# Another PSUM bank for the head outputs, a written TensorE order for the early projections, and fewer weight rests on GpSimd in a two-layer decoder trunk

## The chip, the cores and the metric

The kernel runs on one core of one Trainium2 chip. The metric is the device time of one execution in microseconds (us), less is better. Three executions of the kernel before took 598.71, 599.31 and 599.65 us; their median is 599.31 us.

## The reference

A pre-norm decoder trunk of two layers, batch 1, 256 positions, width 1024, all float32. The even layer projects the normed input once and feeds two groups of heads: A, latent attention (eight heads; a compressed query of 256 and a compressed key/value of 128 columns are normed and projected up, with a rotary part of 32 columns), and B, dilated attention (eight heads of 64). Their outputs go through one output projection. The odd layer is grouped-query attention with a window of 128 and learned sinks (16 query heads, 2 key/value heads). A SwiGLU feed-forward layer of 2816 follows each; a norm ends the trunk.

```python
for layer in range(DEPTH):
    hn = _rmsnorm(h, attn_norm[layer])
    if layer % 2 == 0:
        mix = _even_mixer(hn, ...)   # oA: latent, oB: dilated; concatenate @ w_out
    else:
        mix = _odd_mixer(hn, ...)    # grouped query heads with sinks
    h = h + mix
    h = h + _swiglu(_rmsnorm(h, ffn_norm[layer]), f_w_gate_up[layer], f_w_down[layer])
return _rmsnorm(h, final_norm)
```

In `_even_mixer`, `c_q` and `c_kv` are the first 384 columns of the input projection; `_rmsnorm(c_q) @ w_uq` gives the queries (`pq` in the kernel), `_rmsnorm(c_kv) @ w_ukv` the keys and values (`pk`, `pv`).

## The kernel before, in words

Positions stand on the 128 partitions, in two row blocks `b`. To keep float32 precision, each factor of a product is split in a rounded part `hi` and a **rest** `lo`, and one product is three matmuls (`mm3`, L116): hi·hi (L124), hi·lo (L125), lo·hi (L126), each 128x512 for most weights. A product of this kind is a *job* below.

**Weights** are loaded in units of up to 1 MB into `raw`, three buffers in turn (`load`, L55, on SyncE's queue). `part_weight` (L80) then cuts each unit into parts of up to 512 columns: ScalarE casts `hi` (L93), and `rest` (L73) picks VectorE or GpSimd for the subtraction that makes `lo` (L94). For the seven weights named in `POOLED` (L70) every third rest goes to VectorE and the others to GpSimd; all other rests are VectorE's. `hi` and `lo` lie in seven pairs of buffers.

**Even layer, early part.** `pc` is the product for the latent columns. For each `b` (L231 on): a mean square of the row of `h` gives `rstd_n`, two more of `pc` give `rstd_c` (ScalarE, VectorE, GpSimd in turn), VectorE forms the normed `cg` (L244), TensorE transposes it (`cT`, L252), and a split follows. The dilated projection is a list `bjobs` of 48 jobs, 16 for each of q, k and v; units 0 and 1 of the weight `b` belong to q, 2 and 3 to k, 4 and 5 to v. The first 24 are traced at L307, then `pq`, `pk` and `pv` for each `b`, with the rotary step on `qA` by VectorE for the first half of the heads and by GpSimd for the second (L326 to L331).

**Attention** (`attention`, L452) goes over pairs of heads: four latent (two sets of turns each), four dilated, and eight grouped in the odd layer. Turn `i` of the loop holds: the scores of pair i; the transposes of q and k of pair i+1 (`T`, L433); the transposes of the probabilities of pair i−1 (`pT`, L405), one head after the other; and the head output of pair i−1 (`o`, L416), which is split into `oT`. The remaining jobs fill the places between (`other`, L457): of each share 20, 40 and 60% have been done at the three first places, and the rest at the fourth.

**PSUM** has eight banks. Four (`acc`) rotate for projections; four have names and are used by attention, one buffer each: `s0` and `s1` hold scores (`s0` also the second `pT`), `p` the first `pT`, and `t` both `T` and `o`:

```python
pp = att(("p", "s0")[i], f"pT_{self.name}{i}")   # L403, turn_p
po = att("t", f"o_{self.name}")                  # L410, values
pt = att("t", f"T_{name}")                       # L431, transposes
```

**Order.** A planner orders each engine's instructions by readiness in its own model and by program order. Inside `tc.manual_schedule(engines={PE})` TensorE's order is the one written; before, that held for the two attention loops and the ends of the output projections, not for the early part.

Of the kernel before, what the change touches and what calls it, by code (L numbers as in the profile page):

```python
# [11 lines left out]
F32 = mybir.dt.float32  # L12
F32R = mybir.dt.float32r
# [3 lines left out]
P = 128  # L17
# [23 lines left out]
def trunk(ctx: ExitStack, tc: tile.TileContext, dr):  # L41
    nc = tc.nc
# [24 lines left out]
                between()  # L67
        st["raw"].append((raw, width, cut, u))

    POOLED = {"b", "ukv", "uq", "wo0", "kv", "qc", "wo1"}  # L70
    pooled = [0]

    def rest(name):  # L73

        if name not in POOLED:
            return nc.vector
        pooled[0] += 1
        return nc.vector if pooled[0] % 3 == 0 else nc.gpsimd

    def part_weight(name, between=None):  # L80

        _, n, kts = dr[name]
        st = streams[name]
        raw, width, cut, u = st["raw"].pop(0)
        per = n * kts
        for i in range(width // per):
            hi = wpool.tile([P, 1024], F32R, tag="wh", name=f"wh_{name}_{u}_{i}")
            lo = wpool.tile([P, 1024], F32R, tag="wl", name=f"wl_{name}_{u}_{i}")
            step = min(per, cut, 512 if per == 1024 else 416)
            for a in range(0, per, step):  # L90
                e = min(per, a + step)
                part = raw[:, i * per + a : i * per + e]
                nc.scalar.copy(hi[:, a:e], part)  # L93
                rest(name).tensor_sub(lo[:, a:e], part, hi[:, a:e].bitcast(F32))  # L94
                if between and a == 0 and i == 0:
                    between()
            st["pieces"].append(Piece(hi, lo, n))
# [129 lines left out]
    load("ukv")  # L227
    nc.sync.dma_start(rope, dr["rope"].rearrange("p (b t f) -> p b t f", b=2, t=3))
    nc.sync.dma_start(mask, dr["mask"])
    cT, kr = [], []  # L230
    for b in range(2):  # L231
        rstd.append(row_rstd(b, "n0"))
        sc = small.tile([P, 2], F32, tag="sc", bufs=2, name=f"sc{b}")
        for j, n in enumerate((256, 128)):
            nc.vector.tensor_scalar_mul(sc[:, j : j + 1], rstd[b], 1.0 / math.sqrt(n))
        ms = small.tile([P, 2], F32, tag="ss2", name=f"ssc{b}")
        mean_squares(pc[b][:, 0:256], sc[:, 0:1], ms[:, 0:1], f"cq{b}")
        mean_squares(pc[b][:, 256:384], sc[:, 1:2], ms[:, 1:2], f"ckv{b}")
        r = rsqrt_eps(ms, f"c{b}")
        r2 = small.tile([P, 2], F32, tag="r2", bufs=2, name=f"r2{b}")  # L240
        nc.vector.tensor_scalar_mul(r2, r, rstd[b])
        cg = big.tile([P, 512], F32, tag="big", name=f"cg{b}")
        for j, (a, e) in enumerate(((0, 256), (256, 384))):
            nc.vector.scalar_tensor_tensor(  # L244
                out=cg[:, a:e], in0=pc[b][:, a:e], scalar=r2[:, j : j + 1], in1=gqkv[:, a:e],
                op0=ALU.mult, op1=ALU.mult,
            )
        c = small.tile([P, 32], F32, tag="krn", bufs=2, name=f"krn{b}")
        nc.scalar.activation(c, pc[b][:, 384:416], AF.Copy, scale=rstd[b])
        pt = any_att(f"cT{b}")  # L250
        for j in range(3):
            nc.tensor.transpose(pt[:, j * P : (j + 1) * P], cg[:, j * P : (j + 1) * P], ident)  # L252
        hi = big.tile([P, 512], F32R, tag="big", name=f"cTh{b}")
        lo = big.tile([P, 512], F32R, tag="big", name=f"cTl{b}")
        split(pt[:, :384], hi[:, :384], lo[:, :384])
        cT.append((hi, lo))
        krb = small.tile([P, 32], F32, tag="kr", bufs=2, name=f"kr{b}")
        t = [small.tile([P, 16], F32, tag="krt", bufs=4, name=f"krt{b}{i}") for i in range(2)]
        cos, nsin, sin = (rope[:, b, i, 0:16] for i in range(3))
        x1, x2 = c[:, 0:16], c[:, 16:32]  # L260
        nc.gpsimd.tensor_mul(krb[:, 0:16], x1, cos)
        nc.gpsimd.tensor_mul(krb[:, 16:32], x2, cos)
        nc.gpsimd.tensor_mul(t[0], x2, nsin)
        nc.gpsimd.tensor_mul(t[1], x1, sin)
        nc.gpsimd.tensor_add(krb[:, 0:16], krb[:, 0:16], t[0])
        nc.gpsimd.tensor_add(krb[:, 16:32], krb[:, 16:32], t[1])
        kr.append(krb)
# [36 lines left out]

    qkvB = [[None, None] for _ in range(3)]
    bjobs = project("b", lambda j: 4 * j, 2, range(3), qkvB, rstd, "b", (2,))
    for f in bjobs[:24]:  # L307
        f()

    qA = [[None, None], [None, None]]  # L310
# [2 lines left out]
    for b in range(2):  # L313
        for half in range(2):
            pq = acc(f"pq{b}{half}")
            for kt in range(2):
                mm3(pq[:, :384], ckt(b, kt), piece("uq", kt).at(0, half * 384, (half + 1) * 384), kt == 0, kt == 1)
            t = big.tile([P, 512], F32, tag="big", name=f"qA{b}{half}")
            qA[b][half] = t[:, :384].rearrange("p (h f) -> p h f", f=96)
            nc.scalar.copy(t[:, :384], pq[:, :384])  # L320
            r = qA[b][half]
            x1, x2 = r[:, :, 64:80], r[:, :, 80:96]
            cos, nsin, sin = (rope[:, b, i, :].rearrange("p (h f) -> p h f", f=16) for i in range(3))
            eng = nc.gpsimd if half else nc.vector
            tt = [work.tile([P, 4, 16], F32, tag="ropet", bufs=4, name=f"ropet{b}{half}{i}") for i in range(2)]
            eng.tensor_mul(tt[0], x2, nsin)  # L326
            eng.tensor_mul(tt[1], x1, sin)
            eng.tensor_mul(x1, x1, cos)
            eng.tensor_mul(x2, x2, cos)
            eng.tensor_add(x1, x1, tt[0])  # L330
            eng.tensor_add(x2, x2, tt[1])  # L331
        pk = acc(f"pk{b}")
        mm3(pk, ckt(b, 2), piece("ukv", 0).at(0, 0, 512), True, True)
        for half in range(2):
            t = big.tile([P, 512], F32, tag="big", name=f"kA{b}{half}")
            kA[b][half] = t[:, :384].rearrange("p (h f) -> p h f", f=96)
            nc.scalar.copy(
                kA[b][half][:, :, 0:64],
                pk[:, half * 256 : (half + 1) * 256].rearrange("p (h f) -> p h f", f=64),
            )  # L340
            nc.vector.tensor_copy(kA[b][half][:, :, 64:96], kr[b].unsqueeze(1).to_broadcast([P, 4, 32]))
        pv = acc(f"pv{b}")
        mm3(pv, ckt(b, 2), piece("ukv", 0).at(0, 512, 1024), True, True)
        vA[b] = [big.tile([P, 512], F32R, tag="big", name=f"vA{p}{b}") for p in "hl"]
        split(pv, *vA[b])

# [12 lines left out]
    class Pair:  # L361
# [45 lines left out]
            split(pp[:, :384], hi, lo)  # L407

        def values(self, kt):
            po = att("t", f"o_{self.name}")  # L410
            out = po.rearrange("p (i q) -> p i q", i=2)
            ph, pl = (t.rearrange("p (i q) -> p i q", i=2) for t in self.p)
            for b, q in ((0, slice(0, 256)), (1, slice(256, 384))):
                vh, vl = self.v(b)
                for j, (x, y) in enumerate(((vh, ph), (vl, ph), (vh, pl))):
                    nc.tensor.matmul(  # L416
                        out[:, :, 128 * b : 256], x, y[:, :, q], start=b == 0 and j == 0, stop=b == 1 and j == 2)
            o = big.tile([P, 512], F32R, tag="big", name=f"oT_{self.name}")
            for i in range(2):
                rows = slice(64 * i, 64 * i + 64)  # L420
                split(po[rows, 256 * i : 256 * i + 256], o[rows, 0:256], o[rows, 256:512])
            oT[kt] = o
# [29 lines left out]
    def attention(pairs, fill):  # L452


        n = len(pairs)

        def other(i, part):  # L457
            share = fill[i]
            cuts = [round(len(share) * x) for x in (0, 0.2, 0.4, 0.6, 1)]
            for f in share[cuts[part] : cuts[part + 1]]:  # L460
                f()

        with tc.manual_schedule(engines={mybir.EngineType.PE}):
            for t in pairs[0].turns():
                t()
            for i in range(n + 1):
                ahead = pairs[i + 1].turns() if i + 1 < n else []
                if i < n:
                    pairs[i].scores()
                other(i, 0)  # L470
                for t in ahead[:1]:
                    t()
                if i > 0:
                    pairs[i - 1].turn_p(0)
                other(i, 1)
                for t in ahead[1:]:
                    t()
                if i > 0:
                    pairs[i - 1].turn_p(1)
                other(i, 2)  # L480
                other(i, 3)
                if i > 0:
                    pairs[i - 1].values(i - 1)

# [352 lines left out]
```

## Time and profile before

| | |
|---|---|
| median of three runs | 599.31 us (598.71 to 599.65) |
| the profiled execution's own time | 599.46 us |
| its span | 597.7 us |
| mean granted TensorE clock | 0.989 of full speed |
| HBM read | 100.02 MB |

The profile names engines PE (TensorE), PEld (its weight loads), DVE (VectorE), ACT (ScalarE), POOL (GpSimd) and SP (SyncE). An idle time in brackets is that of the engine just before the instruction, with what ended it. A row that merges several instructions has the time from the first start to the last end. Ends of matmuls are modelled, so the distance between starts says more than a duration. The stages: early part to about 55 us, even attention to 126, first feed-forward layer to 316, qkv of the odd layer to 340, odd attention to 400, second feed-forward layer to the end.

### The profile page before, as it was taken

The numbers are of one execution on the slowest core, as the hardware profiler recorded it, in microseconds if no ns is written. First come the engines' busy times: TensorE is split into PE (matmuls) and PEld (weight loads), VectorE is DVE, ScalarE is ACT, GpSimd is POOL, SyncE is SP. The second block draws the span as 40 slices with busy tenths as digits, with TensorE's granted clock in tenths as the row PEclk, the third lists the DMA queues.
The fourth block names the chain that finished last, engine by engine and source line by source line (L and its number), as shares of the span: only waits on it lengthen the run. The fifth ranks groups of instructions, "written<-read, shape, count | busy, mean of one in ns | idle before, by whom it ended". The sixth has DMA issues, their size and how long they took to land.

```text
span 597.7 us, 7692 instructions
## 1 busy us (share of the span) xinstructions
PE 567.3 (95%) x2661; PEld 461.5 (77%) x2661; DVE 354.3 (59%) x723; ACT 337.9 (57%) x732; POOL 120.4 (20%) x182
## 2 busy tenths in 40 slices
PE   7877998999999999999999899899999999999995
PEld 5655877778888888888888677778888888888884
DVE  5367467787566556554447566778655655554424
ACT  5666678665554555544338677757555555553412
POOL 1697654200000000000037675211000000000000
PEclk9997999999999999999999999999999999999998
DMA  8846525326645545546544634224654554655401
GB/s 257 333 146 250 187 70 178 106 71 247 210 150 204 200 162 202 183 170 212 192 160 144 241 126 167 81 71 138 250 197 161 205 180 173 211 166 188 140 1 70
DMA packets 18183, 101.57 MB, mean 170 GB/s; under 512 B 2272, under 2 KB 3168, under 8 KB 7520
## 3 DMA queue, kind: packets, MB, share of 16 engines
q1 hardware_dynamic: 17712, 100.55, 49.2%
q10 hardware_dynamic: 432, 0.53, 0.2%
q8 instruction: 21, 0.34, 0.2%
q14 instruction: 18, 0.15, 0.1%
HBM read 100.02 MB, written 1.05 MB: 169 GB/s over the span
## 4 chain that ended last, share of the span: by engine, by line
PE 79%; DVE 7%; ACT 5%; DMA 3%; issue 3%; POOL 1%; SPq 0%; POOLq 0%; DVEq 0%; ACTq 0%
PE f1g L126 7%; PE f0g L126 7%; PE f1g L124 7%; PE f0g L124 7%; PE f0g L125 7%; PE f1g L125 7%; PE f0d L124 3%; PE f0d L126 3%; PE f0d L125 3%; PE f1d L126 3%; PE f1d L124 3%; PE f1d L125 3%; DMA raw_b<-in_w_b_dram 2%; PE p L124 2%; PE p L125 2%
## 5 line engine op out<-in xcount | busy, mean ns | idle before, releaser
L94 DVE TENSOR_TENSOR wl_gu<-raw_gu,wh_gu 128x512 fp32r<-128x512 f32 x176 | 115.4, 688 | 68.3 <-ACT wh_gu L93 66.6
L93 ACT CAST wh_gu<-raw_gu 128x512 fp32r<-128x512 f32 x176 | 102.2, 619 | 77.8 <-PE f1g L126 34.7
L94 DVE TENSOR_TENSOR wl_dn<-raw_dn,wh_dn 128x512 fp32r<-128x512 f32 x88 | 57.5, 689 | 54.8 <-ACT wh_dn L93 54.7
L93 ACT CAST wh_dn<-raw_dn 128x512 fp32r<-128x512 f32 x88 | 50.8, 619 | 61.6 <-PE f1d L126 23.3
L124 PE MATMUL f0g<-wh_gu,hTh_p 128*128 128x512 f32 x176 | 69.8, 396 | 0.0
L124 PE MATMUL f1g<-wh_gu,hTh_p 128*128 128x512 f32 x176 | 69.7, 396 | 0.0
L126 PE MATMUL f1g<-wh_gu,hTl_p 128*128 128x512 f32 x176 | 68.8, 391 | 0.0
L126 PE MATMUL f0g<-wh_gu,hTl_p 128*128 128x512 f32 x176 | 68.7, 391 | 0.0
L125 PE MATMUL f0g<-wl_gu,hTh_p 128*128 128x512 f32 x176 | 68.5, 389 | 0.0
L125 PE MATMUL f1g<-wl_gu,hTh_p 128*128 128x512 f32 x176 | 68.5, 389 | 0.0
L126 PEld LDWEIGHTS f0g<-wh_gu,hTl_p 128*128 128x128 f32 x176 | 33.0, 188 | 7.4 <-DVE hTl_p L142 0.4
L126 PEld LDWEIGHTS f1g<-wh_gu,hTl_p 128*128 128x128 f32 x176 | 33.0, 188 | 7.4 <-DVE hTl_p L142 0.4
L125 PEld LDWEIGHTS f1g<-wl_gu,hTh_p 128*128 128x128 f32 x176 | 33.1, 188 | 6.5
L125 PEld LDWEIGHTS f0g<-wl_gu,hTh_p 128*128 128x128 f32 x176 | 33.1, 188 | 6.5
L736 POOL TENSOR_TENSOR rstd_fin<-tot,mhalf 128x1 f32<-128x1 f32 x2 | 1.1, 548 | 183.2 <-DVE tot L732 183.2
L124 PEld LDWEIGHTS f0g<-wh_gu,hTh_p 128*128 128x128 f32 x176 | 33.1, 188 | 6.3
L124 PEld LDWEIGHTS f1g<-wh_gu,hTh_p 128*128 128x128 f32 x176 | 33.1, 188 | 6.3
L124 PE MATMUL f0d<-wh_dn,f0fTh 128*128 128x512 f32 x88 | 34.5, 392 | 0.0
L124 PE MATMUL f1d<-wh_dn,f1fTh 128*128 128x512 f32 x88 | 34.3, 390 | 0.0
L126 PE MATMUL f0d<-wh_dn,f0fTl 128*128 128x512 f32 x88 | 34.3, 390 | 0.0
L126 PE MATMUL f1d<-wh_dn,f1fTl 128*128 128x512 f32 x88 | 34.2, 389 | 0.0
L125 PE MATMUL f1d<-wl_dn,f1fTh 128*128 128x512 f32 x88 | 34.2, 389 | 0.0
(304 smaller groups left out, 1191.8 us busy)
## 6 DMA issues: line engine op xcount, KB each, us to landing
raw_gu<-in_w_gu_dram SPq DMA_DIRECT2D x44, 1024.0 KB, 4.9
raw_dn<-in_w_dn_dram SPq DMA_DIRECT2D x22, 1024.0 KB, 4.8
raw_wo<-in_w_wo_dram SPq DMA_DIRECT2D x8, 1024.0 KB, 5.0
raw_b<-in_w_b_dram SPq DMA_DIRECT2D x4, 1024.0 KB, 6.1
raw_qc<-in_w_qc_dram SPq DMA_DIRECT2D x4, 1024.0 KB, 4.9
bias<-in_bias_dram SPq DMA_DIRECT2D x12, 256.0 KB, 3.8
raw_b<-in_w_b_dram SPq DMA_DIRECT2D x4, 512.0 KB, 6.8
gain<-in_gains_dram SPq DMA_DIRECT2D x4, 512.0 KB, 3.5
```

Of the source, the lines that this page charges most:

```text
L93: nc.scalar.copy(hi[:, a:e], part)
L94: rest(name).tensor_sub(lo[:, a:e], part, hi[:, a:e].bitcast(F32))
L124: nc.tensor.matmul(out, ah, wh, start=first, stop=False)
L125: nc.tensor.matmul(out, ah, wl, start=False, stop=False)
L126: nc.tensor.matmul(out, al, wh, start=False, stop=last)
L736: nc.gpsimd.tensor_tensor(out=r, in0=tot, in1=mhalf[:, :1], op=ALU.pow)
```

## The change

It does three things. Head outputs go to bank `p` instead of `t`. TensorE's order is written down from the first dilated job on (`early`): 12 jobs, the transposes of `cT` for both row blocks, 4 jobs, `pq` for both blocks, `pk` and `pv` for both, 8 jobs; within the attention loops a share is laid out by number (three jobs or two before `T`, one between if the share has over four, the remainder behind the second `pT`) instead of by percentage. And `ukv`, `uq`, `kv` and the units below 3 of `b` and `qc` no longer send rests to GpSimd.

```diff
--- before.py
+++ after.py
@@ -67,12 +67,12 @@
                 between()
         st["raw"].append((raw, width, cut, u))
 
-    POOLED = {"b", "ukv", "uq", "wo0", "kv", "qc", "wo1"}
+    POOLED = {"b", "wo0", "qc", "wo1"}
     pooled = [0]
 
-    def rest(name):
-
-        if name not in POOLED:
+    def rest(name, u):
+
+        if name not in POOLED or (name in ("b", "qc") and u < 3):
             return nc.vector
         pooled[0] += 1
         return nc.vector if pooled[0] % 3 == 0 else nc.gpsimd
@@ -91,7 +91,7 @@
                 e = min(per, a + step)
                 part = raw[:, i * per + a : i * per + e]
                 nc.scalar.copy(hi[:, a:e], part)
-                rest(name).tensor_sub(lo[:, a:e], part, hi[:, a:e].bitcast(F32))
+                rest(name, u).tensor_sub(lo[:, a:e], part, hi[:, a:e].bitcast(F32))
                 if between and a == 0 and i == 0:
                     between()
             st["pieces"].append(Piece(hi, lo, n))
@@ -227,7 +227,7 @@
     load("ukv")
     nc.sync.dma_start(rope, dr["rope"].rearrange("p (b t f) -> p b t f", b=2, t=3))
     nc.sync.dma_start(mask, dr["mask"])
-    cT, kr = [], []
+    cT, kr, cgs = [], [], []
     for b in range(2):
         rstd.append(row_rstd(b, "n0"))
         sc = small.tile([P, 2], F32, tag="sc", bufs=2, name=f"sc{b}")
@@ -247,13 +247,7 @@
             )
         c = small.tile([P, 32], F32, tag="krn", bufs=2, name=f"krn{b}")
         nc.scalar.activation(c, pc[b][:, 384:416], AF.Copy, scale=rstd[b])
-        pt = any_att(f"cT{b}")
-        for j in range(3):
-            nc.tensor.transpose(pt[:, j * P : (j + 1) * P], cg[:, j * P : (j + 1) * P], ident)
-        hi = big.tile([P, 512], F32R, tag="big", name=f"cTh{b}")
-        lo = big.tile([P, 512], F32R, tag="big", name=f"cTl{b}")
-        split(pt[:, :384], hi[:, :384], lo[:, :384])
-        cT.append((hi, lo))
+        cgs.append(cg)
         krb = small.tile([P, 32], F32, tag="kr", bufs=2, name=f"kr{b}")
         t = [small.tile([P, 16], F32, tag="krt", bufs=4, name=f"krt{b}{i}") for i in range(2)]
         cos, nsin, sin = (rope[:, b, i, 0:16] for i in range(3))
@@ -304,7 +298,19 @@
 
     qkvB = [[None, None] for _ in range(3)]
     bjobs = project("b", lambda j: 4 * j, 2, range(3), qkvB, rstd, "b", (2,))
-    for f in bjobs[:24]:
+    early = ExitStack()
+    early.enter_context(tc.manual_schedule(engines={mybir.EngineType.PE}))
+    for f in bjobs[:12]:
+        f()
+    for b in range(2):
+        pt = any_att(f"cT{b}")
+        for j in range(3):
+            nc.tensor.transpose(pt[:, j * P : (j + 1) * P], cgs[b][:, j * P : (j + 1) * P], ident)
+        hi = big.tile([P, 512], F32R, tag="big", name=f"cTh{b}")
+        lo = big.tile([P, 512], F32R, tag="big", name=f"cTl{b}")
+        split(pt[:, :384], hi[:, :384], lo[:, :384])
+        cT.append((hi, lo))
+    for f in bjobs[12:16]:
         f()
 
     qA = [[None, None], [None, None]]
@@ -329,6 +335,7 @@
             eng.tensor_mul(x2, x2, cos)
             eng.tensor_add(x1, x1, tt[0])
             eng.tensor_add(x2, x2, tt[1])
+    for b in range(2):
         pk = acc(f"pk{b}")
         mm3(pk, ckt(b, 2), piece("ukv", 0).at(0, 0, 512), True, True)
         for half in range(2):
@@ -343,6 +350,9 @@
         mm3(pv, ckt(b, 2), piece("ukv", 0).at(0, 512, 1024), True, True)
         vA[b] = [big.tile([P, 512], F32R, tag="big", name=f"vA{p}{b}") for p in "hl"]
         split(pv, *vA[b])
+    for f in bjobs[16:24]:
+        f()
+    early.close()
 
 
 
@@ -407,7 +417,7 @@
             split(pp[:, :384], hi, lo)
 
         def values(self, kt):
-            po = att("t", f"o_{self.name}")
+            po = att("p", f"o_{self.name}")
             out = po.rearrange("p (i q) -> p i q", i=2)
             ph, pl = (t.rearrange("p (i q) -> p i q", i=2) for t in self.p)
             for b, q in ((0, slice(0, 256)), (1, slice(256, 384))):
@@ -454,31 +464,31 @@
 
         n = len(pairs)
 
-        def other(i, part):
-            share = fill[i]
-            cuts = [round(len(share) * x) for x in (0, 0.2, 0.4, 0.6, 1)]
-            for f in share[cuts[part] : cuts[part + 1]]:
+        def other(i, k):
+            for f in fill[i][:k]:
                 f()
+            del fill[i][:k]
 
         with tc.manual_schedule(engines={mybir.EngineType.PE}):
             for t in pairs[0].turns():
                 t()
             for i in range(n + 1):
                 ahead = pairs[i + 1].turns() if i + 1 < n else []
+                many = len(fill[i])
                 if i < n:
                     pairs[i].scores()
-                other(i, 0)
+                other(i, 3 if many > 5 else 2)
                 for t in ahead[:1]:
                     t()
                 if i > 0:
                     pairs[i - 1].turn_p(0)
-                other(i, 1)
+                if many > 4:
+                    other(i, 1)
                 for t in ahead[1:]:
                     t()
                 if i > 0:
                     pairs[i - 1].turn_p(1)
-                other(i, 2)
-                other(i, 3)
+                other(i, many)
                 if i > 0:
                     pairs[i - 1].values(i - 1)
```

## Rows read from the trace of the kernel before

**Rows 1.** The page: busy time by engine; the commonest rest on VectorE.
```profile
...
PE 567.3 (95%) x2661; PEld 461.5 (77%) x2661; DVE 354.3 (59%) x723; ACT 337.9 (57%) x732; POOL 120.4 (20%) x182
...
L94 DVE TENSOR_TENSOR wl_gu<-raw_gu,wh_gu 128x512 fp32r<-128x512 f32 x176 | 115.4, 688 | 68.3 <-ACT wh_gu L93 66.6
...
```

**Rows 2.** Busy time by stage: window, length, busy us of each engine, granted clock, DMA.
```profile
...
19.00:33.00 14.00, 11.91 (x52) 8.88 (x51) 5.75 (x17) 8.58 (x23) 9.38 (x10) 1.00 0.63 244
33.00:45.00 12.00, 9.00 (x38) 6.56 (x37) 7.84 (x11) 7.42 (x17) 12.00 (x23) 0.99 0.53 184
45.00:60.00 15.00, 11.43 (x40) 8.91 (x41) 11.44 (x28) 9.87 (x25) 10.80 (x17) 0.73 0.70 252
...
```

**Rows 3.** The list of PE's waits, whole span: us in total, times, longest.
```profile
...
PE T_a L433 <- DVE qA L330: 5.1, 2, 2.6
PE T_c L433 <- DVE oT_c L142: 3.7, 5, 0.8
...
PE T_kC L433 <- DVE kz0l L142: 1.4, 1, 1.4
PE T_b L433 <- DVE oT_a L142: 1.3, 2, 0.8
...
PE hT_f L600 <- DVE hg_f L595: 0.8, 1, 0.8
...
PE T_b L433 <- DVE oT_b L142: 0.5, 1, 0.5
PE o_b L416 <- DVE kz0l L142: 0.5, 1, 0.5
...
```

**Rows 4.** Timeline of PE, 9 to 62 us: start, us, engine, line, instruction.
```profile
...
16.34 0.40 PE L124 MATMUL b<-wh_b,xTh 128*128 128x512 f32 x1
...
28.84 0.40 PE L124 MATMUL b<-wh_b,xTh 128*128 128x512 f32 x1
...
29.54 0.39 PE L124 MATMUL b<-wh_b,xTh 128*128 128x512 f32 x1
...
55.15 0.66 PE L433 MATMUL T_a<-ident,qA 128*96 128x128 f32 x2 [0.92 <-ACT qk_a L503]
...
```

**Rows 5.** Timelines of DVE, POOL and the chain that ended last, 15 to 35 us.
```profile
...
21.69 0.15 DVE L206 TENSOR_SCALAR ss_n<-ss_n 128x1 f32<-128x1 f32 x1 [1.13 <-ACT junk_n L213]
...
31.45 0.74 DVE L244 SCALAR_TENSOR_TENSOR cg<-c,r,gqkv 128x256 f32<-128x256 f32 x2
...
15.74 8.45 POOL L94 TENSOR_TENSOR wl_b<-raw_b,wh_b 128x512 fp32r<-128x512 f32 x6 [12.59 <-ACT wh_b L93]
24.15 0.56 POOL L207 TENSOR_TENSOR rstd_n<-ss_n,mhalf 128x1 f32<-128x1 f32 x1
...
34.87 4.86 DMA raw_b<-in_w_b_dram
...
```

**Rows 6.** Groups of instructions by form, DVE, 14 to 60 us: busy, mean ns.
```profile
...
L329 DVE TENSOR_TENSOR qA<-qA,rope 128x64 f32<-128x64 f32 x2 | 2.6, 1298 | 0.0
...
L328 DVE TENSOR_TENSOR qA<-qA,rope 128x64 f32<-128x64 f32 x2 | 0.7, 356 | 0.0
...
```

**Rows 7.** PE by window: length, busy us, granted clock, DMA share, GB/s.
```profile
...
45.20:48.20 3.00, 3.00 (x9) 0.50 0.93 373
...
55.10:61.90 6.80, 6.75 (x21) 0.50 0.76 247
...
```

**Rows 8.** Timelines of PE and DVE, one turn of the odd loop.
```profile
...
374.06 0.28 PE L443 MATMUL s_c<-kz1h,qT_c 128*128 128x256 f32 x1
...
376.76 0.41 PE L433 MATMUL T_c<-ident,qCs 128*128 128x128 f32 x2 [0.79 <-DVE oT_c L142]
377.01 0.49 PE L405 MATMUL pT_c<-ident,e_c 128*128 128x128 f32 x3
...
378.03 0.49 PE L405 MATMUL pT_c<-ident,e_c 128*128 128x128 f32 x3
...
378.90 1.02 DVE L142 TENSOR_TENSOR pTl_c<-pT_c,pTh_c 128x384 fp32r<-128x384 f32 x2 [0.20 <-ACT pTh_c L141]
...
```

## The prediction

> **What bounds the kernel now.** I read the page first: over the whole span TensorE (PE) is busy for 95% of the time, VectorE (DVE) for 59% [rows 1]. The feed-forward layers keep PE full, so nothing is to be had there; the change can only win PE's idle time and its slow clock elsewhere. The table of stages comes next: from 19 to 60 us PE has 32.3 us of work in 41, its clock falls to a mean of 0.73 in the last 15 us, and GpSimd (POOL) is busy for 32.2 us of the 41 [rows 2]. The list of PE's waits names the holders [rows 3]: 5.1 us for the rotary step on `qA`, 3.7 and 1.8 us for head outputs `oT` to be read, 0.5 us for `kz0l`, 2.2 us in the qkv stage of the odd layer. A difference of 0.2% (1.2 us) is about what a measurement of this kernel can tell from none.
>
> The forecast is that most of these waits go. The profiled execution took 599.46 us, 1.76 more than its span of 597.7 and 0.15 over the median of 599.31; I sum against 599.46 and take the 0.15 off at the end.
>
> **Part 1: the early order, up to the second transposes of pair 0.** That is one path, so I lay it out anew instead of adding waits. Before, PE starts the dilated jobs at 16.34 and reaches pair 0's second transposes at 55.15 [rows 4]. A job is three matmuls; the first matmuls of two neighbours stand 0.70 apart, so 0.69. Work in the new written order: 24 jobs 16.6; six `cT` transposes 0.6; eight jobs of `pq` at 384 of 512 columns (0.52 each) 4.2; four of `pk` and `pv` 2.8; one set of turns 0.45. Sum 24.6, so 40.9 us if nothing waits.
>
> What waits: the transposes of `cT` for both row blocks now stand together behind 12 jobs, which end at 16.34 + 8.3 = 24.6. The second needs `cg` of block 1, which ended at 32.2 [rows 5]. Its chain runs ScalarE, VectorE, GpSimd in turn, and GpSimd took up `rstd_n` at 24.15 though its input was ready at 21.84, because six rests `wl_b` (8.45 us) stood in its queue [rows 5]. The change takes these rests off GpSimd, so the chain is 2.3 us earlier: 29.9. PE waits 29.9 − 24.6 − 0.3 (the first `cT`) = 5.0 us; this is a new wait, with four jobs, `pq` and all that follows queued behind it. Then 45.9, plus 1.0 for the copies out of the one bank that two sets of turns share (PE sits idle 0.92 for them now [rows 4]): second transposes at 46.9 instead of 55.15, **8.2 us won**.
>
> The rotary step no longer stands in front of PE. It is 12 instructions on VectorE; of one shape, some last 1.30 us, while rests run on GpSimd, and others 0.36 [rows 6]. Eight jobs (5.5 us) and `pk`/`pv` (2.8) now lie between `pq` and its reader. At 0.36 the step is 4.3 us, hidden; with half of them at 1.30, as now, it is 10.0 and shares VectorE with `kA`, `vAl` and unit 2's rests, and up to 3 us would show. Unit 3 of the dilated weights keeps its rests on GpSimd, so I charge 1.0.
>
> The clock, by the rows: after the first wait on `qA`, 2.6 us, PE ran at 0.50 for 3.0 us from 45.2; after the next two waits at 0.50 from 55.1 to 61.9 [rows 3, 7]. The stretch from 55.1 costs 6.8 / 2 = 3.4 and goes with its cause. The new wait of 5.0 us is longer than those that lowered the clock, so it will bring a slow stretch of its own: 1.5 to 3.4, taken as 2.4. Net **+1.0**. The Trainium skill, TensorE: Matmul & The Clock Gate, "HAM oscillation", speaks against this order: one long wait throttles the array and the following work starts cold, so collecting the waits in one place has its price. By it alone the sum would hold the upper price, 3.4; the trace agrees as to the fall, and shows both lengths of it.
>
> Early sum: 8.2 + 1.0 − 1.0 = **8.2 us** (bounds 2 to 12).
>
> **The rests that move.** Early, the code cuts 18 rests for the weights named (12 in units 0 to 2 of `b`, four of `uq`, two of `ukv`); each third is on VectorE already, so 12 move there. A 128x512 one takes 0.69 us on VectorE [rows 1] and 8.45 / 6 = 1.41 on GpSimd [rows 5], so VectorE gets 9 × 0.69 + 3 × 0.56 = 7.9 us (three are of `uq`, 416 columns). It has 41 − 25.0 = 16.0 us idle between 19 and 60 [rows 2], and its own two-input operations get shorter; I cost it at nothing, hidden by that idle time; without it, up to 7.9. The transfers do not move on SyncE's queue, but the buffers of units 0 and 1 come free earlier, so `uq` and `ukv` start a little earlier. Unit 3's load now starts at 34.87 and takes 4.9 us [rows 5]; its first job follows the second transposes (47), so it may start some 5 us later before PE waits. In the odd layer three rests of `kv` and about eight of `qc` move likewise; `T_kC` (1.4) and `hT_f` (0.8) wait for VectorE work stretched by GpSimd [rows 3]. Between 2.2 and nothing: **1.5**, nearer the rows, since VectorE also gets the extra rests.
>
> **Part 2: the bank of the head outputs.** Now `T` of the pair after next waits until `oT` has been read out of bank `t`: 1.3 + 0.5 even, 3.7 odd; `o_b` waits 0.5 because `kz0l` is still being read from `t` [rows 3]. With `o` in `p` the next user of that bank is the first `pT`, two or three jobs, the scores and `T` later. By 0.23 us for 512 columns [rows 4] the scores are 1.04, two jobs 1.38, the two transposes 0.25 (376.76 to 377.01) [rows 8]: 2.7 us. In the odd loop `T` now starts 2.70 us after the head output is through (374.06 to 376.76) [rows 8], so the reading is over in just that time: no margin. Won: **2.3 even**, where four transposes make it 2.9, **3.0 odd** (bounds 1 and 1 below; 2.3 and 3.7 above).
>
> **Part 3: the new shares.** The number of jobs is the same; their places differ. Behind the second `pT` stood four jobs with a share of six, three with five, two with four; now always two, 1.4 us before `o` and 0.5 more to its third matmul, the first that reads `pTl`. In the odd loop, where two jobs stand there already, the three transposes of the second `pT` start at 378.03 and are through some 0.25 later, and `pTl` ends at 379.92, 1.6 us on [rows 8]: it fits by 0.3 us. Nothing is hidden by much there, so I charge **−1.0** (0 to −3) for waits that come up.
>
> **Sum:** 8.2 + 1.5 + 2.3 + 3.0 − 1.0 = 14.0; 599.46 − 14.0 − 0.15 = **585.3 us**. Best case: 12 + 2.2 + 2.3 + 3.7 = 20.2, and 3 more if the statistics of block 1 no longer queue behind block 0's: 576. Worst of this case: 2 + 0 + 1 + 1 − 3 = 1, so 598.
>
> **Rivals.**
> 1. *The fixed order stalls.* Rests on VectorE get in front of the statistics (four at 0.69, 2.8 us later), and PE runs at 0.50 for 6.8 us twice, as it did once: early gain 8.2 + 3.4 − 2.8 − 6.8 = 2.0. Time 599.3 − (2.0 + 1.5 + 2.3 + 3.0 − 1.0) = 591.5. For: the wait of 5 us is certain unless ScalarE's order changes. Against: one slow stretch followed each wait, and behind `cT` PE has 16 us of work.
> 2. *The bank does not do what it is for:* the wait for `oT` moves from `T` to the first `pT`. Then 5.3 is not won: 590.6. For: there is no margin in the odd loop; against: ScalarE and VectorE take up `oT` late now because its reader `T` is late too, and what they do in between is partly rests of later weights.
> 3. *Slower: the splits become the bound in the attention loops.* Place: `o` behind the second `pT`. Cover lost: 2 jobs in four latent pairs (5.5 us), one in four dilated (2.8), and the one between the two `pT` in some six grouped (4.1): 12.4, and then the 5.3 of the bank is not seen either, as ScalarE and VectorE set the pace. 599.3 − 8.2 − 1.5 + 12.4 = 602. It decides once the split lasts over 1.9 us after the second `pT`; it lasts 1.6 now [rows 8].
>
> **How the numbers follow.** Forecast 0.58, rival 1 0.17, rival 2 0.14, rival 3 0.08, no change that shows 0.03. Faster by over 0.2%: 0.88; within: 0.03; slower: 0.09 (rival 3, and a hundredth for early losses beyond rival 1). The range takes in the forecast's best case and rivals 1 and 2 with some room: 576.5 to 595.5. The forecast's own range is 576.5 to 590.
>
> **What would show it.** Right: `rstd_n` starts by 22.5; one PE wait on `cg` of 4 to 5 us near 25, with a slow clock behind it; second transposes of pair 0 near 47 to 49; no wait of `T` on `oT`; rotary instructions at 0.36. Wrong: a wait on `qA` as long as before, PE waits of `o` on `pTl` or of `pT` on `oT` in each pair, or VectorE without gaps from 20 to 47.

## The result and the profile after

The kernel after takes **590.56 us**, the median of four runs (589.34 to 591.01), against 599.39 us for the kernel before beside it: a ratio of **0.9851** (95% interval 0.9833 to 0.9869), so 8.8 us less. The forecast was 585.3. The result lies inside the range of 576.5 to 595.5, on the predicted side, but 0.6 us above the forecast's own range (576.5 to 590) and with 8.8 of the 14.0 us that were summed up. The profiled execution took 591.01 us, with a span of 589.2 and a mean granted clock of 0.992.

Busy time by engine, on the page of the kernel after:

```profile
PE 567.2 (96%) x2661; PEld 461.3 (78%) x2661; DVE 360.9 (61%) x746; ACT 337.0 (57%) x732; POOL 93.4 (16%) x159
```

PE's work is what it was [rows 1]; GpSimd has 27 us less, VectorE 6.6 more. The same stages as in [rows 2] (columns: length, busy us of PE, PEld, DVE, ACT, POOL, granted clock, DMA):

```profile
19.00:33.00 14.00, 9.64 (x40) 7.51 (x39) 7.37 (x22) 8.07 (x21) 5.34 (x16) 0.92 0.86 337
33.00:45.00 12.00, 12.00 (x56) 10.30 (x55) 9.35 (x24) 10.95 (x25) 6.17 (x13) 0.95 0.45 175
45.00:60.00 15.00, 12.26 (x58) 9.67 (x57) 11.20 (x21) 9.36 (x24) 14.40 (x15) 0.89 0.64 215
```

The idle time has moved forward: PE now idles in the first stage, where the new wait is, and has no gap at all in the second. The list of PE's waits over the whole span (us in total, times, longest):

```profile
PE cT L308 <- DVE cg L244: 4.4, 2, 3.5
PE T_a L443 <- ACT qk_a L513: 2.7, 2, 2.5
...
PE s_a L524 <- ACT qk_a L513: 0.9, 1, 0.9
PE o_c L426 <- DVE pTl_c L142: 0.9, 3, 0.3
PE p L124 <- ACT oT_b L141: 0.8, 1, 0.8
PE p L124 <- ACT oT_c L141: 0.8, 1, 0.8
...
PE T_kC L443 <- DVE kz0l L142: 0.6, 1, 0.6
...
PE pT_c L415 <- DVE oT_c L142: 0.2, 1, 0.2
```

Every wait of [rows 3] that the change aims at is gone or short: none of `T` on `qA`, none of `T` on `oT`, and only 0.2 us of `pT` on `oT`. In their place stand `cT` (the new wait that the prediction priced), `T_a` on the copy `qk_a`, and 0.8 us at the end of each attention loop (0.4 and 0.3 before). PE's timeline, at the transposes of `cT` and of pair 0 (the dilated jobs start at 16.32, [rows 4] had 16.34):

```profile
26.13 0.52 PE L308 MATMUL cT<-ident,cg 128*128 128x128 f32 x3 [0.83 <-DVE cg L244]
30.18 0.59 PE L308 MATMUL cT<-ident,cg 128*128 128x128 f32 x3 [3.53 <-DVE cg L244]
...
47.59 0.38 PE L443 MATMUL T_a<-ident,qA 128*96 128x128 f32 x2
50.72 0.42 PE L443 MATMUL T_a<-ident,qA 128*96 128x128 f32 x2 [2.53 <-ACT qk_a L513]
```

The granted clock around the two waits (PE by window: length, busy us, granted clock, DMA share, GB/s):

```profile
29.00:30.50 1.50, 0.32 (x3) 1.00 0.93 355
30.50:34.20 3.70, 3.70 (x12) 0.54 0.10 34
34.20:47.50 13.30, 13.30 (x64) 1.00 0.58 217
...
50.90:54.50 3.60, 3.60 (x14) 0.54 0.73 237
```

Behind each of the two long waits PE runs at about half clock (1.2 GHz) for 3.6 to 3.7 us. The second wait is the one that the prediction did not have. What stood before the copy `qk_a` on VectorE, and what GpSimd did meanwhile, one fence each:

```profile
44.57 1.98 DVE L348 COPY kA<-kr 128x128 f32<-128x128 f32 x2
...
47.07 2.86 DVE L94 TENSOR_TENSOR wl_b<-raw_b,wh_b 128x512 fp32r<-128x512 f32 x2
49.85 0.41 DVE L512 COPY qk_a<-T_a 96x256 f32<-96x256 f32 x1
```

```profile
22.24 0.56 POOL L207 TENSOR_TENSOR rstd_n<-ss_n,mhalf 128x1 f32<-128x1 f32 x1 [19.09 <-DVE ss_n L206]
...
43.63 8.65 POOL L94 TENSOR_TENSOR wl_b<-raw_b,wh_b 128x512 fp32r<-128x512 f32 x6 [0.73 <-ACT wh_b L93]
```

GpSimd is free when `ss_n` comes, so `rstd_n` starts at 22.24 instead of 24.15 [rows 5]. From 43.63 it works on six rests of the units from 3 on, and two rests of the same weight on VectorE last 1.43 us each in that time instead of 0.69 [rows 1]. The copy `qk_a`, on which PE waits, stands behind them. VectorE's queue has no slack here, as the window ahead of the copy shows (columns as in the table of stages):

```profile
36.25:50.30 14.05, 11.94 (x58) 9.91 (x56) 14.01 (x28) 10.93 (x25) 11.47 (x17) 1.00 0.67 238
```

VectorE is busy for 14.01 of 14.05 us, and the profile's chain to the second transposes runs through it from 36.77 on. Some 4.6 us of that are rests of `ukv` and of unit 2 of `b`, most of which the change moved there.

To see where time came from, I take the starts of a few PE instructions out of each kernel's timeline and subtract: up to the first head output `o_a`; the even loop from there to the first gate product `f0g`; from there to the odd layer's first `o_c`; the odd loop to `f1g`; the rest of the span. Of the variants below, each is one profiled execution, and those of `undo_rests`, `undo_bank`, `undo_shares` and `loops_only` took 1.5 to 2.8 us more than their medians, so their first column is read with care; the later columns agree to a tenth or two between kernels that share the code of that stage.

```
                 first o_a   even loop   ffn + qkv   odd loop   rest
before             72.77       58.87      219.99      53.24     192.8
after              67.92       58.36      218.06      52.13     192.7
undo_rests         73.57       58.31      219.96      51.55     192.7
undo_order         66.54       58.30      218.03      52.09     192.7
undo_bank          70.66       61.34      218.05      51.39     192.8
undo_shares        70.37       58.71      218.08      55.30     192.7
rests_only         66.98       59.41      218.05      53.98     192.7
loops_only         74.06       58.29      220.00      51.55     192.8
no_b_rests         67.00       58.31      218.04      52.08     192.8
tail_t             68.01       57.60      218.09      51.37     192.7
cover_cT           63.48       59.67      218.09      52.19   192.8
cover_both         64.05       58.42      218.10      52.12     192.7
cover_all          63.59       57.71      218.11      51.41     192.8
cover_all_no_b     61.94       57.66      218.10      51.38     192.7
```

So the early part gave 4.85 us (forecast 8.2), the two attention loops 0.5 and 1.1 (forecast, with the charge for the shares, 4.3 together), the qkv stage 1.9 (forecast 1.5).

### The profile page after: what moved, and what is told of

It reads as the page before. It is cut to its first block, busy times and chain, and to the rows that moved or that the text cites. A ratio compares the mean times of both kernels' runs of the same rounds, so it can differ in the third digit from the quotient of the medians.

```text
span 589.2 us, 7680 instructions
## 1 busy us (share of the span) xinstructions
PE 567.2 (96%) x2661; PEld 461.3 (78%) x2661; DVE 360.9 (61%) x746; ACT 337.0 (57%) x732; POOL 93.4 (16%) x159
## 4 chain that ended last, share of the span: by engine, by line
PE 79%; DVE 8%; ACT 6%; issue 3%; DMA 2%; POOL 1%; SPq 1%; POOLq 0%; DVEq 0%; ACTq 0%
PE f1g L126 7%; PE f0g L126 7%; PE f0g L124 7%; PE f1g L124 7%; PE f1g L125 7%; PE f0g L125 7%; PE f0d L126 3%; PE f0d L125 3%; PE f0d L124 3%; PE f1d L124 3%; PE f1d L125 3%; PE f1d L126 3%; PE p L124 2%; DMA h<-in_x_dram 1%; PE p L125 1%
## 5 line engine op out<-in xcount | busy, mean ns | idle before, releaser
L125 PE MATMUL f0d<-wl_dn,f0fTh 128*128 128x512 f32 x88 | 34.2, 389 | 0.0
```

Of the source, the lines that this page charges most:

```text
L125: nc.tensor.matmul(out, ah, wl, start=False, stop=False)
```

## Experiments

First, each part is taken out of the change alone.

**undo_rests**: the changed kernel with the old division of rests.

```diff
-    POOLED = {"b", "wo0", "qc", "wo1"}
+    POOLED = {"b", "ukv", "uq", "wo0", "kv", "qc", "wo1"}
...
-        if name not in POOLED or (name in ("b", "qc") and u < 3):
+        if name not in POOLED:
```

> The changed kernel with the old rule for rests (GpSimd takes two of three for all seven weights). Theory A (the gain comes from the early stretch and the qkv stage, and there from rests leaving GpSimd's queue): the first rstd_n starts again near 24.1 us instead of 22.2, the second cT waits 2 us longer, kC and hT_f waits come back (1.9 us); 594 to 596 us. Rival (rests are worth nothing, VectorE only got fuller): 590 to 591 us.

Measured: 595.61 us, ratio 0.9942 (0.9918 to 0.9965). The division of the rests is therefore worth 0.0091, about **5.4 us**, the largest part of the change. In the table it stands in two places: the first head output and the qkv stage, 219.96 as in the kernel before instead of 218.06. `rstd_n` starts at 24.23 again, and the waits for `kz0l` and `hg_f` are back (1.4 and 0.8 us). The second `cT` does not wait 2 us longer, as expected, but 3.54 us as in the kernel after: the first one is later too, and the two stay 4.1 us apart. The odd loop is 0.6 us shorter with the old division; the reason for that was not followed up.

**undo_order**: the changed kernel without the written order of the early part (planner's order as before; the `cT` transposes back in their loop, and `pq`, `pk` and `pv` by row block again, for all engines).

```diff
-    early = ExitStack()
-    early.enter_context(tc.manual_schedule(engines={mybir.EngineType.PE}))
-    for f in bjobs[:12]:
+    for f in bjobs[:24]:
         f()
...
```

> The changed kernel without the written early order (cT in its old place, pq, pk and pv by row block, TensorE ordered by the planner up to attention). Theory A (the order hides the rotary step and is worth some 3 us net of its own 4.4 us wait on cg): 593 to 595 us, with T_a waiting on qA again. Rival (once rests are off GpSimd the rotary step is short anyway, and the order only collects waits): 588 to 590.6 us.

Measured: 590.13 us, ratio 0.9840 (0.9818 to 0.9863): no difference from 0.9851 with the order, as the intervals overlap. The written order, as it was made, brings no gain that these runs can tell. PE's waits in this variant:

```profile
PE T_a L433 <- DVE qA L330: 3.7, 1, 3.7
PE T_a L433 <- ACT qk_a L503: 1.5, 2, 0.9
...
PE cT L252 <- DVE cg L244: 1.3, 2, 0.7
```

Its wait for the rotary step is still there, 3.7 us, and the order does remove it. But the planner puts other jobs between the two `cT`, and waits 1.3 us there where the written order waits 4.4. The rotary step behind the wait, and GpSimd beside it:

```profile
41.70 1.30 DVE L326 TENSOR_TENSOR ropet<-qA,rope 128x64 f32<-128x64 f32 x1
...
44.15 1.30 DVE L329 TENSOR_TENSOR qA<-qA,rope 128x64 f32<-128x64 f32 x1
45.37 0.35 DVE L328 TENSOR_TENSOR qA<-qA,rope 128x64 f32<-128x64 f32 x1
```

```profile
39.94 5.43 POOL L94 TENSOR_TENSOR wl_b<-raw_b,wh_b 128x512 fp32r<-128x512 f32 x4
```

The instructions take 1.30 us until GpSimd's rests end at 45.37, and 0.35 from then on, beside GpSimd's own rotary instructions of 0.32 us. That is the pair of lengths of [rows 6] with its cause beside it; with GpSimd idle the same instructions take 0.22 us (37.31 to 38.07 in this trace). In the Trainium skill, SBUF — State Buffer, "Who interferes with whom", a VectorE instruction with two inputs in the state buffer contends with a GpSimd instruction that reads it; this trace agrees.

**undo_bank**: head outputs back in bank `t`, all else as changed.

```diff
-            po = att("p", f"o_{self.name}")
+            po = att("t", f"o_{self.name}")
```

> The changed kernel with head outputs back in bank t. Theory A (the bank takes the wait of T on oT away, at the price of about 1 us in the last turns of each attention loop, where pT now meets o in p): T waits 0.1 to 0.5 us per turn even with the new shares, last turns shorter by 0.9 us each; net 591.5 to 593.5 us. Rival (the wait only moved to o and pT): 589.5 to 590.6 us.

Measured: 594.33 us, ratio 0.9906 (0.9885 to 0.9928). What it costs stands in the even loop (61.34 instead of 58.36), and the waits name it:

```profile
PE o_a L426 <- DVE kz0l L142: 2.0, 1, 2.0
...
PE o_b L426 <- DVE kz1l L142: 1.4, 1, 1.4
...
PE o_b L426 <- DVE kz0l L142: 1.1, 1, 1.1
```

Expected was a wait of `T`; it is `o` that waits, and the time is above the expected 591.5 to 593.5. With `o` in `t`, the head output waits until the transposes of q and k have been read out of `t`. In the odd loop nothing is lost; it is 0.7 us shorter. There, `T` no longer waits for `oT` even without the new bank: the new shares, with two jobs and the scores ahead of `T`, are enough. The first column (2.7 us later) cannot be a wait of head outputs, as none has run by then. In that execution one rest `wl_wo` of VectorE's lasted 4.21 us and the copy `qk_a` stood behind it; 1.65 us of it is that execution's distance to the median.

**undo_shares**: the percentages back, all else as changed.

```diff
-        def other(i, k):
-            for f in fill[i][:k]:
+        def other(i, part):
+            share = fill[i]
+            cuts = [round(len(share) * x) for x in (0, 0.2, 0.4, 0.6, 1)]
+            for f in share[cuts[part] : cuts[part + 1]]:
                 f()
-            del fill[i][:k]
...
```

> The changed kernel with the old shares (20, 40, 60% of each share). Theory A: with one job instead of two ahead of T, o has 2.0 us to be read out of p before the first pT and needs 2.7; pT waits about 0.7 us in each grouped turn; 592.5 to 594.5 us. Rival (more jobs behind the second pT cover the split better): 589 to 590.6 us.

Measured: 594.24 us, ratio 0.9915 (0.9891 to 0.9939). The odd loop takes 55.30 instead of 52.13. The wait and one of its six places:

```profile
PE pT_c L415 <- DVE oT_c L142: 4.2, 6, 1.2
```

```profile
365.88 0.52 PE L415 MATMUL pT_c<-ident,e_c 128*128 128x128 f32 x3 [1.17 <-DVE oT_c L142]
```

This is rival 2 as a mechanism: with the new bank and the old shares the wait for `oT` does not go, it moves from `T` to the first `pT`. The changed shares are what puts two jobs in front of it. Part 2 of the change works only together with part 3.

**rests_only** and **loops_only**: the kernel before with the new division of rests alone, and with the new bank and shares alone.

```diff
rests_only = before.py
+    POOLED = {"b", "wo0", "qc", "wo1"}
...
+        if name not in POOLED or (name in ("b", "qc") and u < 3):
loops_only = before.py
+            po = att("p", f"o_{self.name}")
...
+        def other(i, k):
...
+                other(i, 3 if many > 5 else 2)
...
+                other(i, many)
```

> The kernel before with the new rule for rests alone. Theory A (rests are the largest part and act alone: earlier statistics, short rotary step, qkv stage): 593.5 to 595 us. Rival (rests pay only with the written order): 597 to 599 us.

> The kernel before with the bank and the shares alone. Theory A (rests and the loops add up; the loops are worth 8.8 - 5.4 = 3.4 us): 595 to 597 us. Rival (the loops gain only because the early stretch and its queues are shorter): 598 to 599.4 us.

Measured: 592.93 us, 0.9884 (0.9865 to 0.9904), and 596.94 us, 0.9952 (0.9933 to 0.9971): 7.0 and 2.9 us less than before. Together that makes 9.8, and undo_order, which is both, has 9.6: within the intervals the two parts add up, and nothing is left that could be put down to the order. (rests_only is somewhat under the expected 593.5 to 595.) In rests_only `T` waits for `qA` once instead of twice, and the waits on `oT` remain:

```profile
PE T_c L433 <- DVE oT_c L142: 4.5, 5, 1.4
PE T_a L433 <- DVE qA L330: 3.7, 1, 3.7
```

**no_b_rests**: the changed kernel with no rest of weight `b` on GpSimd (units 3 to 5), to see what the charge of 1.0 us for unit 3 should have been.

```diff
-    POOLED = {"b", "wo0", "qc", "wo1"}
+    POOLED = {"wo0", "qc", "wo1"}
```

> The changed kernel with no rest of the dilated weights on GpSimd (units 3 to 5 too). Theory A (what is left of the early stretch is unit 3's rests on GpSimd: they hold the copies, the rotary step and VectorE's own rests of unit 3, 1.43 us each instead of 0.69, in front of the copies out of bank t): second transposes of pair 0 near 48.9 us instead of 50.7 and a shorter slow-clock stretch after them; 2 to 3.5 us off, 587 to 588.5 us. Rival (VectorE gets fuller by eight rests and is late as before): 590 to 592 us.

Measured: 590.38 us, ratio 0.9846 (0.9827 to 0.9864): no difference from the changed kernel. The step in itself does what it should; VectorE and then PE, one fence each, and PE's windows:

```profile
44.67 3.68 DVE L94 TENSOR_TENSOR wl_b<-raw_b,wh_b 128x512 fp32r<-128x512 f32 x6
48.28 0.41 DVE L512 COPY qk_a<-T_a 96x256 f32<-96x256 f32 x1
```

```profile
49.14 0.42 PE L443 MATMUL T_a<-ident,qA 128*96 128x128 f32 x2 [1.75 <-ACT qk_a L513]
```

```profile
50.60:57.00 6.40, 6.31 (x18) 0.50 0.79 274
```

A rest is back to 0.61 us, the second transposes stand at 49.14 instead of 50.72, and the wait is 0.8 us shorter. But six rests now stand in front of the copy, PE still waits 1.75 us, and behind that it runs at 0.50 for 6.4 us instead of at 0.54 for 3.6. Of the expectation, the transposes came (48.9), the shorter slow stretch did not, and the time is in the rival's range. At 0.50 instead of 0.54, and for longer, the slow clock costs 3.2 us instead of 1.7 and takes back most of what the shorter waits gave: the first head output is 0.9 us earlier, and the median does not show it. So the next variants put work into the waits.

**tail_t**: the last two turns of each loop put the head output in `t` again, where nothing needs it by then.

```diff
-            po = att("p", f"o_{self.name}")
+            po = att("t" if kt >= 6 else "p", f"o_{self.name}")
```

> The changed kernel with the head outputs of the last two pairs of each attention loop back in bank t, where no transposes of q and k follow. Theory A (the bank costs about 0.9 us at the end of each loop: pT meets o in p, the planner puts a job of the output projection ahead of it, and that job is missing behind the last head output): about 1.8 us off, 588.5 to 589.5 us, the waits of p on oT back from 0.8 to 0.3 us. Rival (the tail is bound by something else): 590.5 us.

Measured: 589.59 us, ratio 0.9823 (0.9804 to 0.9842). Against the changed kernel (0.9851) the intervals overlap, but both loops are 0.8 us shorter in the table, just at their ends. The end of the odd loop in the kernel after, and then in tail_t:

```profile
388.51 0.63 PE L426 MATMUL o_c<-pTh_c,vC 128*128 128x512 f32 x2
...
391.44 0.50 PE L124 MATMUL p<-wh_wo,oT_c 128*128 128x512 f32 x1 [0.77 <-ACT oT_c L141]
```

```profile
387.12 0.63 PE L426 MATMUL o_c<-pTh_c,vC 128*128 128x512 f32 x2
...
390.04 0.51 PE L124 MATMUL p<-wh_wo,oT_c 128*128 128x512 f32 x1 [0.30 <-ACT oT_c L141]
```

From the last head output to the output projection that needs it are 2.9 us in both, the time to read it out. In tail_t six matmuls of jobs lie in those 2.9 us, in the kernel after four; there the head output shares its bank with `pT`, and the other two (0.46 us) stand ahead of the last `pT`, where eight matmuls run instead of six. That is 0.5 of the 0.8 us; the remainder was not traced.

Then the two early waits are filled with jobs instead of being made shorter.

**cover_cT**: the four jobs behind the second `cT` go between the two.

```diff
+        if b == 0:
+            for f in bjobs[12:16]:
+                f()
-    for f in bjobs[12:16]:
-        f()
```

> The changed kernel with the four dilated jobs put between the two row blocks' transposes of cT instead of behind them. Theory A (the written order gains nothing because its own wait on cg of 3.5 us, and the 1.2 GHz stretch behind it, give back what it hides): the second wait falls to about 1.0 us, no slow stretch behind it, first transposes of pair 0 near 43.5 us instead of 47.6; time lower by up to 4.4 us if what follows keeps up, so 586 to 588.5 us. Rival (TensorE only arrives earlier at the copies out of bank t, which VectorE reaches when it does): 590 to 591 us, with the wait of T_a on qk_a longer by what cT lost.

Measured: 588.20 us, ratio 0.9816 (0.9796 to 0.9836). The wait for `cg` falls from 4.4 to 2.3 us; a new one of 1.4 comes up, `pq` for the cast `wh_uq`, since `pq` now comes earlier. The time is in the expected range, but two of its marks are not met: a slow stretch is still there (0.51 from 33.9 to 37.4, behind waits of 0.76 and 1.44 us), and the first transposes of pair 0 stand at 46.63, not near 43.5. The first head output is 4.4 us earlier than in the kernel after, and the even loop takes 1.3 us of that back.

**cover_both**: also, the last four early jobs go between the two sets of transposes of pair 0, where PE waits for the copy.

```diff
-    for f in bjobs[16:24]:
+    for f in bjobs[16:20]:
...
-            for t in pairs[0].turns():
-                t()
+            first, *rest_turns = pairs[0].turns()
+            first()
+            for f in pre:
+                f()
+            for t in rest_turns:
+                t()
...
+        shares((6, 6, 6, 6, 5, 5, 5, 5, 4), bjobs[24:] + out0.jobs(range(6))), bjobs[20:24])
```

> cover_cT, and the last four of the early dilated jobs stand between the two sets of transposes of pair 0. Theory A (the order pays once both of its waits stand behind work): no wait over 1.5 us between 20 and 60 us, granted clock 1.0 from 30 to 55, 583 to 586.5 us. Rival (VectorE's queue is the bound there): 588 to 590 us, T_a still waits on qk_a.

Measured: 586.08 us, ratio 0.9780 (0.9758 to 0.9802). The first head output comes at 64.05 instead of 67.92. The time came as expected, but not its marks: PE still waits for `qk_a`, one step later, and a slow stretch is there, though not behind that wait (PE's waits, then its windows):

```profile
PE s_a L529 <- ACT qk_a L518: 2.1, 1, 2.1
...
PE pq L124 <- ACT wh_uq L93: 1.4, 1, 1.4
```

```profile
32.70:35.90 3.20, 3.16 (x9) 0.50 0.17 23
50.70:55.00 4.30, 4.10 (x20) 1.00 0.69 227
```

The slow stretch follows the wait of 1.44 us before 32.74; behind the 2.06 us that end at 50.68 the clock stays at full speed. Against undo_order (0.9840) the kernel with the order and both fills is faster by 0.006 or 3.6 us. That this is the written order's is not shown: the second fill lies in the attention loop, whose order is written in undo_order too, and undo_order with that fill alone was not run; cover_cT, the order with the first fill, does not stand clear of undo_order (0.9816 against 0.9840, the intervals overlap).

**cover_all**: cover_both with the bank of tail_t. **cover_all_no_b**: that, with no rest of `b` on GpSimd.

```diff
cover_all = cover_both
+            po = att("t" if kt >= 6 else "p", f"o_{self.name}")
cover_all_no_b = cover_all
+    POOLED = {"wo0", "qc", "wo1"}
```

> cover_both with the head outputs of the last two pairs in bank t. Theory A (the three add up): 1 to 1.8 us under cover_both, 582 to 585 us. Rival: no difference to cover_both.

> cover_all with no rest of the dilated weights on GpSimd. Theory A (two rests of unit 3 on VectorE, 1.56 us each beside GpSimd's, stand in front of the second copy qk_a, and TensorE's wait of 2.0 us for it in the scores is their price; in no_b_rests the slow clock that followed hid this): those rests 0.6 to 0.7 us each, that wait under 1 us, 582.5 to 583.5 us. Rival (VectorE takes eight more rests and loses as much): 584 to 586 us.

Measured: 584.52 us, 0.9748 (0.9729 to 0.9768), and **583.96 us, 0.9743** (0.9725 to 0.9762). The first is in its expected range. The second has the lowest median here, 6.6 us below the change and 15.4 below before. Between these two the medians differ by 0.6 us, which the intervals don't settle; the profiled executions differ by 1.8. The second missed its expected 582.5 to 583.5, and its wait for `qk_a`, expected under 1 us, is 1.41, though the rests are back to 0.62 us each. PE from 20 to 60 us, and its waits, in the second:

```profile
20.00:60.00 40.00, 34.67 (x170) 1.00 0.77 286
```

```profile
PE cT L308 <- DVE cg L244: 1.7, 2, 0.9
PE pq L124 <- ACT wh_uq L93: 1.4, 1, 1.4
PE s_a L529 <- ACT qk_a L518: 1.4, 1, 1.4
```

The waits that are left are 0.8 to 1.4 us each, and in this execution the clock is granted in full throughout. That need not be a property of the variant: this execution has a mean clock of 0.999, the other four have 0.994 or 0.995 and took 583.77 to 584.44 us against its 583.64. In the profiled execution of cover_all, waits of 0.76 and 1.43 us at the same two places (0.77 and 1.43 here) are followed by 3.7 us at 0.54, which costs 1.7 us, so the 1.8 us between the two profiled executions cannot be put down to the rests.

## Why the prediction was right or wrong

**Direction and range: right; the place of the early gain: wrong.** That 590.56 us is rival 2's figure (590.6) is chance, as the wait that rival 2 speaks of takes 0.2 us. These marks were met: `rstd_n` at 22.24 (by 22.5), the wait on `cg` with a slow clock behind it (in two parts, 0.83 and 3.53 us), no wait of `T` on `oT`, and rotary instructions of 0.36 us or less. The same line with GpSimd idle, and then beside GpSimd's rotary instructions:

```profile
37.65 0.22 DVE L335 TENSOR_TENSOR qA<-qA,rope 128x64 f32<-128x64 f32 x1
...
40.20 0.36 DVE L335 TENSOR_TENSOR qA<-qA,rope 128x64 f32<-128x64 f32 x1
```

Not met is the mark of the second transposes of pair 0, near 47 to 49: they stand at 50.72. The first ones stand at 47.59, and the prediction's own terms add up to 50.3. The sign of being wrong, VectorE without gaps from 20 to 47, came in part: from 36.25 on.

**The early sum, 8.2: measured 4.85.** Up to the second transposes of pair 0 the sum held: 46.9, with 2.4 for the new slow stretch and the charge of 1.0, makes 50.3; they stand at 50.72. That it comes so close is in part luck, as its terms miss both ways: the 12 jobs end at 25.3, 0.7 late. Further, the wait for `cg` is 0.83 + 3.53 = 4.4 us against 5.0, and its slow stretch of 3.7 us at 0.54 costs 3.7 × 0.46 = 1.7 against 2.4. By the rule of the Trainium skill, TensorE: Matmul & The Clock Gate, "HAM oscillation", work behind a long wait starts cold: the trace agrees. The upper price of 3.4 that the prediction tied to this rule did not come here. The wait for the copy `qk_a` is 2.53 us against the 1.0 set for it; the charge for unit 3's rests on GpSimd covers most of that, but it was made for the rotary step, which was hidden by then, and the harm came one step later. With it failed a term put at nothing, the rests moved to VectorE, "hidden by that idle time": VectorE has no idle time from 36.25 up to that copy. What share of the 2.53 us is the moved rests' and what share is GpSimd's slowing of VectorE, no run separates; in no_b_rests, with more rests on VectorE and GpSimd without any, the wait is 1.75.

The step that failed is the next one: "the stretch from 55.1 costs 6.8 / 2 = 3.4 and goes with its cause". PE's list of instructions from the second transposes to the first head output is as long as before, 78 records in both windows; it took 17.62 us and takes 17.20. Of 3.4 forecast, 0.4 came. The cause did not go. The copy `qk_a` behind VectorE's slowed rests holds PE for 2.53 us, and behind that the stretch is back, from 50.9, for 3.6 × 0.46 = 1.7 us; further on, PE waits 0.9 us for the copy once more (`s_a`, behind a rest of 1.59 and one of 1.77 us) and 0.2 once. That is 2.8 of the 3.0 us that are missing. Rival 1 had the second slow stretch, but with the statistics late; they were early.

**What the 4.85 comes from.** The prediction tied it to the written order, with only 2.3 us from the rests (the earlier statistics). That reading fell: rests_only has the first head output at 66.98 and undo_order at 66.54, both without the order. Rests off GpSimd make the early part 5.8 us shorter by themselves (66.98 against 72.77); against undo_order, the order removed a wait of 3.7 us on `qA` and the 6.0 us at 0.50 behind it, raised the waits on `cg` from 1.3 to 4.4 and of `T_a` on `qk_a` from 1.5 to 2.7, and put in the two slow stretches of 3.7 and 3.6 us.

**The rests that move:** nothing early and 1.5 in the qkv stage; the stage gave 1.9, with `T_kC` down from 1.4 [rows 3] to 0.6 us and `hT_f` gone from the list. As a part, the rests are worth 5.4 us taken out and 7.0 put in alone, much more than their term, since the gain of the statistics stands in the early sum.

**The bank and the shares, 2.3 + 3.0 − 1.0 = 4.3: measured 1.6.** That the 5.5 us of waits on `oT` go was right, and rival 2 was wrong, but only because the shares changed too: undo_shares shows its mechanism at 4.2 us. The charge of 1.0 was about right in size, as `o` now waits for `pTl`, for 1.4 us in all (0.9 of it `o_c`). Not seen were the ends: when there is no next pair, `o` meets `pT` in bank `p`, and each loop lost 0.8 us there (tail_t shows both), 1.5 in all. Of the 1.2 us then missing, 0.6 lies in the odd loop with the new rests (51.55 in loops_only and undo_rests against 52.13); the rest was not traced further. Rival 3 did not come: `o` waits for `pTl` for 0.3 us at most.

Sum: of the 5.5 us missing (14.0 less 8.5 in the span), 3.35 are early and 2.7 in the loops, less 0.4 and 0.1 that came in addition in the qkv stage and behind the loops.

**Open:** what decides whether a wait is followed by a slow stretch, and whether that is 3.2 or 6.4 us long; what the second fill gives without the written order; whether the last variant is really faster than the one before it; what makes the odd loop 0.6 us longer with the new rests.

## What to carry to other kernels

An order written by hand has to be paid for at its own waits: before it is fixed, look for what each new place waits for and lay independent jobs there, or the planner's order is as good. What PE waits for may stand in another engine's full queue; then an earlier PE only waits longer. Where a two-input operation runs on VectorE and GpSimd at once, count both the slower rest and the short instruction on the critical path queued behind it. A bank that is right for the steady turns of a loop can be wrong for its last turn, which has fewer users in between.

## What was not expected of the hardware

A copy with one input slows down beside GpSimd's rests too: two copies `kA`, 128x128, take 1.98 us beside them (after, at 44.57). In no_b_rests, where GpSimd is idle at that place, one takes 0.21 us, the shortest of the four (min/median/max in ns):

```profile
L348 DVE COPY kA<-kr x4: 210/280/360, 40.5 to 43.9; 128x128 f32<-128x128 f32 x4
```

And the slow stretch does not go by the length of the one wait before it: 2.53 us stand before 3.6 at 0.54 (after), 1.75 before 6.4 at 0.50 (no_b_rests), 1.44 before 3.2 at 0.50 and 2.06 before none (both cover_both), while in the profiled execution of cover_all_no_b a wait of 1.43 at the same place has none behind it.
